# Queueing a block's gate product on VectorE behind that block's own low part

## The chip, the cores and the metric

The kernel runs on one core of a Trainium2 chip. The metric is the device time of one execution in microseconds. Three runs of the kernel before gave 3089.33 to 3090.34 us, median 3090.05 us.

## What is computed

Two small network blocks run one after the other on 256 tokens of width 1024. Each ends, and the second has twice, a "PEER" layer: every token picks 16 of 16384 experts in each of 8 heads, and an expert is a pair of rows, one of a table u and one of a table v.

```python
e = (i1 * PEER_NKEYS + i2).reshape(TOK_BLOCK, PEER_HEADS * K)
gate = jax.nn.softmax(best_s, axis=-1).reshape(TOK_BLOCK, PEER_HEADS * K)
u = expert_u[e]
act = jax.nn.gelu(jnp.einsum('td,ted->te', xb, u), approximate=False)
coef = (gate * act.astype(jnp.float32)).astype(xb.dtype)
return jnp.einsum('te,ted->td', coef, expert_v[e])
```

Between the three PEER layers lie token mixers (a convolution with an RWKV scan, a gated linear attention, a stick-breaking attention), norms and residuals. All is float32.

## The kernel before, in words

**PEER as two dense products.** The kernel does not gather experts. It computes the activation of all 16384 experts for all 256 tokens and multiplies it by a gate that is zero where a token did not pick the expert. In `peer` (L1049) this is done in blocks of 128 experts. The *up stage* (loop at L1189, 128 blocks) multiplies a block of u with the tokens into the PSUM tile `pu`, and ScalarE's Gelu (L1197) writes the result to `C`, an SBUF tile with 256 columns per block. The *down stage* (`vstep`, L1209, and `acc_nat`, L151, 128 blocks) multiplies `C` with the block of v and adds up into the four PSUM tiles `py`, two halves of the tokens by two halves of the width.

**Float32 by three products.** Every streamed operand is split in two parts: `hi`, a rounded copy made by ScalarE (L79 for weights, L106 for activations, where it is called `ch`), and `lo`, the rest, made by VectorE as raw minus hi (L81; L107, called `cl`). A product is hi by hi, hi by lo and lo by hi. In the down stage these are, per block and per tile of `py`, ch by hi (L162), ch by lo (L163) and cl by hi (L164): 12 products of 128x512 per block.

```python
raw = self.sp.tile([128, n], F32, tag="raw", name="raw", bufs=RAW)
nc.sync.dma_start(raw, ap)
...
nc.scalar.copy(hi, raw)
with self.behind():
    self.los.append(nc.vector.tensor_tensor(lo, raw, hi.bitcast(F32), op=OP.subtract))
```

This is `stream` (L72): one block of a table comes by a DMA of SP's queue (512 KB, four `raw` buffers), and `hi` and `lo` have three buffers each, as have `ch` and `cl` in the down stage. `self.los` keeps every lo instruction.

**The gates.** They are found during the up stage by work that is interleaved with it. For the tokens 128 to 255 the gate is multiplied into `C` in the up stage (L1136, L1201). For the tokens 0 to 127 the gates are added into a table `G` in HBM by 128 indirect DMAs on GpSimd (L1097), and the down stage reads it back: for every four blocks `vstep` loads a tile `gate` of 256 KB on GpSimd's queue (L1212, two buffers), and VectorE multiplies it into the first 128 columns of the block in `C` (L1215). This *gate product* must come before the block's ch and cl.

**What sets the order.** A scheduler orders each engine's instructions when the program is built; an engine then runs its own list strictly in order and waits by semaphores. `tc.issue_after(x)` tells the scheduler to put the instructions of its body behind x on their engine. Before, x is `done`, the last lo of the up stage. The last three blocks of the down stage (`TAIL`, L169) are worked off tile by tile of `py`, so that its four tiles finish one after the other.

**Around the stages.** Behind the first and the second down stage come the mixers: SP's queue loads the old residual (`res`, L676) and the mixer's first weights, and GpSimd's queue loads rows for the norm (`rowg`, `rowb`, L669); VectorE adds `py` to `res` (L688, L714). Behind the third one there is only the last norm (L714 to L722) and the output.

Of the kernel before, what the change touches and what calls it, by code (L numbers as in the profile page):

```python
# [39 lines left out]
class Net:  # L40
# [1008 lines left out]
    def peer(self, xh, xl, wq, skT, uT, v, G, Gnext=None, rate=1.5, dve_a=2):  # L1049
# [5 lines left out]
        nc, tc = self.nc, self.tc  # L1055
        V = nc.vector
        NS = 88
        with ExitStack() as ctx:
# [19 lines left out]
            def after(i):  # L1078
                for j in last:
                    tc.add_manual_dep(i.ins, j.ins.name, SYNC, reason="adds of the head before")  # L1080
# [123 lines left out]
            py = [self.ps.tile([128, 512], F32, tag="y", name="py", bufs=4) for i in range(4)]  # L1204
            Gv = G.rearrange("(p b t) o -> p b (t o)", p=128, t=128)
            gate = [None]
            done = self.los[-1]

            def vstep(b):  # L1209
                if b % 4 == 0:  # L1210
                    gate[0] = wp.tile([128, 4, 128], F32, tag="A", name="gate")
                    after(nc.gpsimd.dma_start(gate[0], Gv[:, b:b + 4]))  # L1212
                hi, lo = self.stream(v[b])
                with tc.issue_after(done.ins):
                    V.tensor_tensor(C3[:, b, :128], C3[:, b, :128], gate[0][:, b % 4], op=OP.mult)  # L1215
                ch = wp.tile([128, 256], F32R, tag="ch", name="ch", bufs=TAIL)
                cl = wp.tile([128, 256], F32R, tag="cl", name="cl", bufs=TAIL)
                self.split(ch, cl, C3[:, b])
                return ch, cl, hi, lo
            self.acc_nat(py, range(128), vstep)  # L1220
        return py

# [158 lines left out]
def build(nc, tc, a):  # L1381
    with ExitStack() as ctx:
# [15 lines left out]
        n.block1(a, *x)  # L1398
        nc.gpsimd.dma_start(n.vec2, a["vec2"])
        py = peer(0, x)  # L1400
        x, y = xt(), xt()

        def first_a(fp):
            s = n.load_res(fp, hs[0])
            n.add_rms(fp, s, py, n.rows(fp, a["g_final_row"], "g"), *x, norm=True)
            return s
        n.mixer_a(a, first_a, *x, *y, hs[1])
        py = peer(1, y)
        x, y = xt(), xt()

        def first_b(fp):
            s = n.load_res(fp, hs[1])
            n.add_ln(fp, s, py, a, (0, 1), *x)
            return s
        n.mixer_b(a, first_b, *x, *y, hs[2])
        py = peer(2, y)
        with tc.tile_pool(name="fc", bufs=1) as fp:
            n.add_ln(fp, n.load_res(fp, hs[2]), py, a, (1, 1), dst=a["out"])
# [17 lines left out]
```

## Time and profile before

| | |
|---|---|
| median of three runs | 3090.05 us (3089.33 to 3090.34) |
| the profiled execution's own time | 3088.2 us |
| its span, first to last instruction | 3086.4 us |
| mean granted TensorE clock | 0.987 |
| TensorE products, busy | 2982.7 us (97%), 21313 |
| VectorE, busy | 2101.8 us (68%), 4439 |
| ScalarE, busy | 1621.3 us (53%), 3016 |
| gate product L1215 | 384 of 286 ns, 90.6 us |
| lo L81 | 939, 1141.3 us |
| hi L79 | 939, 978.1 us |

A timeline row gives the start, the duration, the engine, the line and what is written from what; in brackets stands how long the engine had been idle and what ended that. "PE" is TensorE's products, "PEld" its weight loads, which run ahead of the products, "DVE" VectorE, "ACT" ScalarE, "POOL" GpSimd. Products overlap: one of 128x512 has a duration of 0.39 us in the rows, and the next one starts 0.23 us after it. So TensorE can be late without an idle time in its row.

### The profile page before, as it was taken

The numbers are of one execution on the slowest core, as the hardware profiler recorded it, in microseconds if no ns is written. First come the engines' busy times: TensorE is split into PE (matmuls) and PEld (weight loads), VectorE is DVE, ScalarE is ACT, GpSimd is POOL, SyncE is SP. The second block draws the span as 40 slices with busy tenths as digits, with TensorE's granted clock in tenths as the row PEclk, the third lists the DMA queues.
The fourth block names the chain that finished last, engine by engine and source line by source line (L and its number), as shares of the span: only waits on it lengthen the run. The fifth ranks groups of instructions, "written<-read, shape, count | busy, mean of one in ns | idle before, by whom it ended". The sixth has DMA issues, their size and how long they took to land. (4 is left out here: it accounts for less than half of the span.)

```text
span 3086.4 us, 56042 instructions
## 1 busy us (share of the span) xinstructions
PE 2982.7 (97%) x21313; PEld 2716.2 (88%) x21313; DVE 2101.8 (68%) x4439; ACT 1621.3 (53%) x3016; POOL 857.2 (28%) x564
## 2 busy tenths in 40 slices
PE   9999999999899999999999999998999999989998
PEld 8888999999688888899999878887889999978887
DVE  6976997545766665798744666665599764476666
ACT  6345558544455454456844444455544774444554
POOL 0000067884100010008788100000002878610000
PEclk9999999999999999999999999999999999999999
DMA  9745566666756653456666666655345666676665
GB/s 313 231 142 194 178 163 139 171 183 208 244 192 194 195 179 116 156 174 157 144 179 185 231 219 194 195 193 174 112 158 176 147 150 185 190 238 211 194 193 176
DMA packets 231918, 568.83 MB, mean 184 GB/s; under 512 B 74416, under 2 KB 99264, under 8 KB 231392
## 3 DMA queue, kind: packets, MB, share of 16 engines
q1 hardware_dynamic: 165536, 529.31, 52.4%
q0 software_dynamic: 66112, 35.94, 8.2%
q8 instruction: 167, 2.74, 0.4%
q14 instruction: 103, 0.84, 0.1%
HBM read 533.49 MB, written 31.65 MB: 183 GB/s over the span
## 5 line engine op out<-in xcount | busy, mean ns | idle before, releaser
L81 DVE TENSOR_TENSOR lo<-raw,hi 128x1024 fp32r<-128x1024 f32 (+1 forms) x939 | 1141.3, 1216 | 558.3 <-ACT hi L79 553.1
L79 ACT CAST hi<-raw 128x1024 fp32r<-128x1024 f32 (+1 forms) x939 | 978.1, 1043 | 691.0 <-PE pu L112 274.3
L1097 POOL DMA_INDIRECT G<-gts,idx x384 | 774.4, 2017 | 525.2 <-issue 140.2
L111 PE MATMUL pu<-xh,hi 128*128 128x256 f32 x3072 | 879.0, 286 | 3.0 <-ACT hi L79 3.0
L113 PE MATMUL pu<-xh,lo 128*128 128x256 f32 x3072 | 874.2, 285 | 7.4 <-DVE lo L81 7.4
L112 PE MATMUL pu<-xl,hi 128*128 128x256 f32 x3072 | 871.2, 284 | 0.0
L163 PE MATMUL py<-lo,ch 128*128 128x512 f32 x1536 | 602.6, 392 | 32.0 <-DVE lo L81 32.0
L113 PEld LDWEIGHTS pu<-xh,lo 128*128 128x128 f32 x3072 | 590.9, 192 | 11.9 <-DVE lo L81 10.5
L164 PE MATMUL py<-hi,cl 128*128 128x512 f32 x1536 | 598.6, 390 | 0.0
L162 PE MATMUL py<-hi,ch 128*128 128x512 f32 x1536 | 598.5, 390 | 0.0
L111 PEld LDWEIGHTS pu<-xh,hi 128*128 128x128 f32 x3072 | 591.0, 192 | 3.6 <-ACT hi L79 3.6
L112 PEld LDWEIGHTS pu<-xl,hi 128*128 128x128 f32 x3072 | 591.4, 193 | 0.0
L106 ACT CAST ch<-C 128x256 fp32r<-128x256 f32 x384 | 156.1, 407 | 557.6 <-PE py L163 552.1
L163 PEld LDWEIGHTS py<-lo,ch 128*128 128x128 f32 x1536 | 288.7, 188 | 106.9 <-DVE lo L81 47.5
L162 PEld LDWEIGHTS py<-hi,ch 128*128 128x128 f32 x1536 | 288.4, 188 | 61.2 <-ACT hi L79 0.9
L164 PEld LDWEIGHTS py<-hi,cl 128*128 128x128 f32 x1536 | 288.7, 188 | 58.6
L107 DVE TENSOR_TENSOR cl<-C,ch 128x256 fp32r<-128x256 f32 x384 | 162.5, 424 | 162.1 <-ACT ch L106 162.1
L669 POOL DMA_DIRECT2D rowg<-in_ln_rows_dram x4 | 2.2, 551 | 580.9 <-DVE cl L107 560.9
L111 PE MATMUL pz<-xh,hi 128*128 128x256 f32 (+1 forms) x504 | 149.6, 298 | 8.5 <-ACT hi L79 6.1
L113 PE MATMUL pz<-xh,lo 128*128 128x256 f32 (+1 forms) x504 | 147.3, 293 | 1.1 <-DVE lo L81 1.1
L112 PE MATMUL pz<-xl,hi 128*128 128x256 f32 (+1 forms) x504 | 146.7, 291 | 0.5 <-DVE xl L214 0.5
L1215 DVE TENSOR_TENSOR C<-C,gate 128x128 f32<-128x128 f32 x384 | 90.6, 286 | 65.5 <-DMA gate<-G 65.4
(490 smaller groups left out, 3605.3 us busy)
## 6 DMA issues: line engine op xcount, KB each, us to landing
raw<-in_u_dram SPq DMA_DIRECT2D x384, 512.0 KB
raw<-in_v_dram SPq DMA_DIRECT2D x384, 512.0 KB
G<-zero SPq DMA_DIRECT2D x96, 256.0 KB
raw<-in_wq_dram SPq DMA_DIRECT2D x48, 512.0 KB
gate<-G POOLq DMA_DIRECT2D x96, 256.0 KB
raw<-in_w_in_dram SPq DMA_DIRECT2D x38, 512.0 KB
raw<-in_a_w_inT_dram SPq DMA_DIRECT2D x14, 512.0 KB
raw<-in_b_wT_dram SPq DMA_DIRECT2D x14, 512.0 KB
```

The costliest lines, as they stand in the source:

```text
L79: nc.scalar.copy(hi, raw)
L81: self.los.append(nc.vector.tensor_tensor(lo, raw, hi.bitcast(F32), op=OP.subtract))
L106: nc.scalar.copy(hi, src)
L107: nc.vector.tensor_tensor(lo, src, hi.bitcast(F32), op=OP.subtract)
L111: mm(out, lh, rh, start=start, stop=False)
L112: mm(out, lh, rl, start=False, stop=False)
L113: mm(out, ll, rh, start=False, stop=stop)
L162: mm(po[q], xh[:, ts], hi[:, h], start=f, stop=False)
L163: mm(po[q], xh[:, ts], lo[:, h], start=False, stop=False)
L164: mm(po[q], xl[:, ts], hi[:, h], start=False, stop=l)
L1097: i = nc.gpsimd.indirect_dma_start(G, bass.IndirectOffsetOnAxis(ap=idx[:, k:k + 1], axis=0), gts[:, k:k + 1], None, compute_op=OP.add)
L1215: V.tensor_tensor(C3[:, b, :128], C3[:, b, :128], gate[0][:, b % 4], op=OP.mult)
```

## The change

The gate product of block b is put behind the lo of block b, which `stream` has just appended to `self.los`, in place of the last lo of the up stage:

```diff
@@ -1204,14 +1204,13 @@
             py = [self.ps.tile([128, 512], F32, tag="y", name="py", bufs=4) for i in range(4)]
             Gv = G.rearrange("(p b t) o -> p b (t o)", p=128, t=128)
             gate = [None]
-            done = self.los[-1]
 
             def vstep(b):
                 if b % 4 == 0:
                     gate[0] = wp.tile([128, 4, 128], F32, tag="A", name="gate")
                     after(nc.gpsimd.dma_start(gate[0], Gv[:, b:b + 4]))
                 hi, lo = self.stream(v[b])
-                with tc.issue_after(done.ins):
+                with tc.issue_after(self.los[-1].ins):
                     V.tensor_tensor(C3[:, b, :128], C3[:, b, :128], gate[0][:, b % 4], op=OP.mult)
                 ch = wp.tile([128, 256], F32R, tag="ch", name="ch", bufs=TAIL)
                 cl = wp.tile([128, 256], F32R, tag="cl", name="cl", bufs=TAIL)
```

One line goes, so that all later lines have a number less by one: the gate product, L1215 before, is L1214 in the changed kernel. What the scheduler makes of it is shown at three places. The numbers behind the names tell buffers' tiles apart; each block has its own.

The start of the first down stage on VectorE, before; lo_9887 and lo_9910 are those of the down stage's blocks 0 and 1 (L1201 still belongs to the up stage):

```order
L1201 TENSOR_TENSOR C_3873<-C_3873,act_9770 128x128
L1215 TENSOR_TENSOR C_3873<-C_3873,gate_9882 128x128 x4
L107 TENSOR_TENSOR cl_9892<-C_3873,ch_9891 128x256
L1215 TENSOR_TENSOR C_3873<-C_3873,gate_9976 128x128 x3
L81 TENSOR_TENSOR lo_9887<-raw_9884,hi_9886 128x1024
L1201 TENSOR_TENSOR C_3873<-C_3873,act_9805 128x128
L107 TENSOR_TENSOR cl_9915<-C_3873,ch_9914 128x256
L107 TENSOR_TENSOR cl_9938<-C_3873,ch_9937 128x256
L1215 TENSOR_TENSOR C_3873<-C_3873,gate_9976 128x128
L1215 TENSOR_TENSOR C_3873<-C_3873,gate_10070 128x128 x3
L81 TENSOR_TENSOR lo_9910<-raw_9907,hi_9909 128x1024
```

The same place in the changed kernel, behind lo_9887; lo_9933 and lo_9956 are those of blocks 2 and 3:

```order
L1201 TENSOR_TENSOR C_3873<-C_3873,act_9805 128x128
L1214 TENSOR_TENSOR C_3873<-C_3873,gate_9882 128x128
L107 TENSOR_TENSOR cl_9892<-C_3873,ch_9891 128x256
L81 TENSOR_TENSOR lo_9910<-raw_9907,hi_9909 128x1024
L1201 TENSOR_TENSOR C_3873<-C_3873,act_9840 128x128
L1214 TENSOR_TENSOR C_3873<-C_3873,gate_9882 128x128
L107 TENSOR_TENSOR cl_9915<-C_3873,ch_9914 128x256
L1201 TENSOR_TENSOR C_3873<-C_3873,act_9875 128x128
L81 TENSOR_TENSOR lo_9933<-raw_9930,hi_9932 128x1024
L1214 TENSOR_TENSOR C_3873<-C_3873,gate_9882 128x128
L81 TENSOR_TENSOR lo_9956<-raw_9953,hi_9955 128x1024
L107 TENSOR_TENSOR cl_9938<-C_3873,ch_9937 128x256
```

Before, eleven gate products of three gate tiles stand ahead of the second block's lo; now each block has one, and from the third block on cl of a block stands behind lo of the block after it (cl_9938 is block 2's).

ScalarE further on in the first down stage, before; ch_10054, ch_10079 and ch_10102 are those of blocks 7, 8 and 9, hi_10049, hi_10074, hi_10097 and hi_10120 those of blocks 7 to 10:

```order
L106 CAST ch_10054<-C_3873 128x256
L79 CAST hi_10049<-raw_10047 128x1024
L106 CAST ch_10079<-C_3873 128x256
L79 CAST hi_10074<-raw_10072 128x1024
L106 CAST ch_10102<-C_3873 128x256
```

And in the changed kernel:

```order
L106 CAST ch_10054<-C_3873 128x256
L79 CAST hi_10097<-raw_10095 128x1024
L106 CAST ch_10079<-C_3873 128x256
L79 CAST hi_10120<-raw_10118 128x1024
L106 CAST ch_10102<-C_3873 128x256
```

Before, ch of a block came ahead of its own hi; now hi of block 9 comes ahead of ch of block 8. This pattern holds to the end of each down stage.

The end of the first down stage on VectorE, before; cl_12851 and lo_12846 belong to the last block, meml and res to the mixer:

```order
L107 TENSOR_TENSOR cl_12840<-C_3873,ch_12839 128x256
L81 TENSOR_TENSOR lo_12835<-raw_12832,hi_12834 128x1024
L107 TENSOR_TENSOR cl_12851<-C_3873,ch_12850 128x256
L81 TENSOR_TENSOR lo_12846<-raw_12843,hi_12845 128x1024
L107 TENSOR_TENSOR meml_12908<-memr_12909,memh_12907 128x1024
```

And in the changed kernel:

```order
L81 TENSOR_TENSOR lo_12846<-raw_12843,hi_12845 128x1024
L107 TENSOR_TENSOR cl_12840<-C_3873,ch_12839 128x256
L1214 TENSOR_TENSOR C_3873<-C_3873,gate_12796 128x128
L107 TENSOR_TENSOR cl_12851<-C_3873,ch_12850 128x256
L107 TENSOR_TENSOR meml_12908<-memr_12909,memh_12907 128x1024
```

The last cl has moved behind the last lo, the cl of the block before and the last gate product; the third down stage ends in the same order. On SP's queue at the first stage's end, before (a_w_mk and a_w_mv are the mixer's first weights, res the residual):

```order
L75 DMA raw_12918<-in_a_w_mk_dram 128x1024
L676 DMA res_13047<-h0_90 128x1024
L75 DMA raw_12950<-in_a_w_mk_dram 128x1024
L75 DMA raw_12985<-in_a_w_mv_dram 128x1024
L75 DMA raw_13015<-in_a_w_mv_dram 128x1024
L676 DMA res_13049<-h0_90 128x1024
```

And in the changed kernel:

```order
L75 DMA raw_12918<-in_a_w_mk_dram 128x1024
L75 DMA raw_12950<-in_a_w_mk_dram 128x1024
L676 DMA res_13047<-h0_90 128x1024
L676 DMA res_13049<-h0_90 128x1024
L75 DMA raw_12985<-in_a_w_mv_dram 128x1024
L75 DMA raw_13015<-in_a_w_mv_dram 128x1024
```

The two loads of the residual have come together, behind both loads of the first weight.

## Rows read from the trace of the kernel before

**Rows 1.** TensorE's longest wait of the whole program (engine, line, waited for: us, times, longest us).
```profile
PE py L163 <- DVE lo L81: 32.0, 34, 2.2
```

**Rows 2.** Busy time by stretch: the three down stages (columns named in its head).
```profile
core 0: us, PE busy (x) PEld busy (x) DVE busy (x) ACT busy (x) POOL busy (x), PEclk, DMA share, GB/s
750.31:1104.72 354.41, 343.48 (x1503) 280.64 (x1501) 226.96 (x369) 170.09 (x252) 15.02 (x28) 1.00 0.64 207
1729.48:2084.76 355.28, 344.00 (x1503) 280.52 (x1501) 227.36 (x369) 170.10 (x252) 15.03 (x28) 1.00 0.63 207
2713.07:3067.70 354.63, 344.80 (x1502) 281.80 (x1501) 227.19 (x369) 170.34 (x252) 15.02 (x28) 1.00 0.63 204
sum 1064.32, PE 1032.29 PEld 842.95 DVE 681.50 ACT 510.53 POOL 45.07; mean PE 344.10 PEld 280.98 DVE 227.17 ACT 170.18 POOL 15.02
```

**Rows 3.** The same view: an early and a late stretch of the first down stage.
```profile
760.00:860.00 100.00, 89.07 (x380) 69.98 (x379) 72.00 (x169) 42.18 (x63) 12.88 (x24) 1.00 0.72 238
900.00:1000.00 100.00, 100.00 (x443) 82.77 (x442) 60.43 (x74) 50.38 (x74) 0.00 (x0) 1.00 0.60 193
```

**Rows 4.** Timeline of VectorE (start us, us, instruction, [idle before <-releaser]), before a stall.
```profile
760.39 0.50 DVE L1215 TENSOR_TENSOR C<-C,gate 128x128 f32<-128x128 f32 x2 [1.16 <-DMA gate<-G]
760.80 1.22 DVE L81 TENSOR_TENSOR lo<-raw,hi 128x1024 fp32r<-128x1024 f32 x1
```

**Rows 5.** Timeline of TensorE's weight loads at that stall.
```profile
762.08 0.19 PEld L163 LDWEIGHTS py<-lo,ch 128*128 128x128 f32 x1 [0.89 <-DVE lo L81]
```

**Rows 6.** The gate product's line, what it waited for (us, times).
```profile
  DMA gate<-G: 65.4, 46
```

**Rows 7.** Timeline of TensorE, undisturbed blocks and two later places.
```profile
952.17 0.39 PE L164 MATMUL py<-hi,cl 128*128 128x512 f32 x1
952.40 0.39 PE L162 MATMUL py<-hi,ch 128*128 128x512 f32 x1
...
1104.72 0.39 PE L162 MATMUL py<-hi,ch 128*128 128x512 f32 x1
...
2091.62 0.39 PE L164 MATMUL py<-hi,cl 128*128 128x512 f32 x1
```

**Rows 8.** The chain that ended last (start us, us, what): the longest gate transfer on it.
```profile
2685.95 6.63 DMA gate<-G
```

**Rows 9.** Timeline of ScalarE, an undisturbed block and the second stage's end.
```profile
952.68 1.05 ACT L79 CAST hi<-raw 128x1024 fp32r<-128x1024 f32 x1
...
2092.04 1.05 ACT L79 CAST hi<-raw 128x1024 fp32r<-128x1024 f32 x1 [4.06 <-PE py L164]
```

**Rows 10.** Timeline of VectorE, an undisturbed block and the first stage's end.
```profile
952.81 0.42 DVE L107 TENSOR_TENSOR cl<-C,ch 128x256 fp32r<-128x256 f32 x1 [0.54 <-ACT ch L106]
953.76 1.22 DVE L81 TENSOR_TENSOR lo<-raw,hi 128x1024 fp32r<-128x1024 f32 x1 [0.53 <-ACT hi L79]
...
1106.08 1.23 DVE L81 TENSOR_TENSOR lo<-raw,hi 128x1024 fp32r<-128x1024 f32 x1 [0.53 <-ACT hi L79]
1107.23 1.22 DVE L107 TENSOR_TENSOR meml<-memr,memh 128x1024 fp32r<-128x1024 f32 x1
```

**Rows 11.** Timeline of TensorE's weight loads, undisturbed.
```profile
952.63 0.19 PEld L164 LDWEIGHTS py<-hi,cl 128*128 128x128 f32 x1
```

**Rows 12.** Timeline of TensorE's products: the one behind the stalled one.
```profile
762.42 0.40 PE L164 MATMUL py<-hi,cl 128*128 128x512 f32 x1
```

**Rows 13.** The same chain, at the end of the third down stage.
```profile
3068.11 0.44 DVE cl L107
3068.57 3.23 DMA res<-h
3071.92 1.28 DVE res L714 x2
```

**Rows 14.** Timeline of TensorE behind the first and the second down stage.
```profile
1115.57 0.39 PE L111 MATMUL pz<-memh,hi 128*128 128x256 f32 x1 [2.24 <-ACT hi L79]
...
2097.74 0.58 PE L111 MATMUL pz<-memh,hi 128*128 128x256 f32 x1 [4.09 <-ACT hi L79]
```

## The prediction, made before the changed kernel ran

> **What bounds the kernel now.** Look first at who makes TensorE wait. The longest entry of its waits is the product with the block's low part: 34 waits, 32.0 us, all for VectorE's lo [rows 1]. They lie in the down stages, so the next view is the busy time of the three down stages, each taken from its first product to the first product of its last three blocks (125 blocks) [rows 2]: 354.41, 355.28 and 354.63 us. The granted clock is 1.00 in all three. Then compare two stretches inside a stage: from 760 to 860 us TensorE is busy 89.07 of 100 us, from 900 to 1000 us all of it [rows 3]. The loss is thus at the stage's start, where the gate products run.
>
> The mechanism is in VectorE's timeline around one stall: two gate products had to wait 1.16 us for their gate transfer, and behind them in VectorE's queue stood a lo that waited for nothing else; it ended at 760.80 + 1.22 = 762.02 us [rows 4]. TensorE's weight load for the product with that lo starts at 762.08 us [rows 5]. In the whole program gate products waited 65.4 us for gate transfers, 46 times [rows 6]. Before the change, products of later blocks are queued as early as a scheduler finds room, and a product that nobody needs yet holds up a lo that TensorE needs now.
>
> An undisturbed block takes 2.72 us: from 952.40 to 1104.72 us are 56 blocks, 152.32 / 56 [rows 7]. 125 blocks without a stall are 340.0 us, three stages 1020.0; measured are 1064.32 [rows 2]. So the stalls and the restarts behind them cost **44.3 us**, more than the 32.0 us of idle time, since each also delays the products behind it.
>
> **The change, part by part.** Nothing is added or removed: 384 gate products, 96 gate transfers, all casts stay. Their places move.
>
> *Products.* Each product now stands behind its own block's lo, and so block by block through the stage. A product has the gate of its four blocks loaded while the buffer before is used up: two buffers, so a transfer may be issued once the last product of a group is done, and is needed five blocks later, 5 x 2.72 = 13.6 us. The longest gate transfer on the chain took 6.63 us [rows 8]. I cost gate waits at nothing; the cover is 7 us. DMA load: gate bytes no longer come in a burst of 238 GB/s [rows 3] but spread at 256 KB per four blocks, 10.9 us, some 24 GB/s on top of the 193 of the quiet stretch [rows 3], 217 in all. That is less than the burst carried, so nothing. Gain: 44.3 us, if nothing takes the stalls' place.
>
> *The order that the scheduler now makes.* This is where the gain can be lost. Before, a block's ch and cl are made first and its hi and lo after. Now ScalarE makes hi of block b+1 ahead of ch of block b, and VectorE lo of b+1 ahead of cl of b. hi has three buffers, so hi of b+1 can start only when TensorE has finished block b-2. I follow that chain from S, the start of block b-1's first product:
> - TensorE's last product of b-2 starts 0.23 us before S (952.17 against 952.40 [rows 7]); a hi that waited for such a product started 0.42 us after its start (2091.62 [rows 7], 2092.04 [rows 9]). hi of b+1 starts at S + 0.19.
> - hi to lo, start to start: 952.68 [rows 9] to 953.76 [rows 10], 1.08. lo of b+1 starts at S + 1.27.
> - lo to the next instruction: 1106.08 to 1107.23, 1.15 [rows 10]. cl of b starts at S + 2.42 and takes 0.42 (the row at 952.81 [rows 10]): S + 2.84. Its ch is done before: behind hi, at about S + 1.56.
> - VectorE's end to TensorE's weight load 0.06 (762.02 to 762.08 [rows 4, 5]): usable at **S + 2.90**.
> - Due: block b starts at S + 2.72, and the weight load of cl 0.23 later (952.63 [rows 11] against 952.40), **S + 2.95**. It may be late by a little: undisturbed the matmul after its own starts 0.45 us behind it (952.40 + 3 x 0.227 = 953.08), behind the late load at 762.08 it started at 762.42 [rows 12], 0.34. So 0.11 us are hidden, and the limit is S + 3.06.
>
> The chain fits by 0.16 us. Before there was more than a block of reserve: the lo that ended at 953.76 + 1.22 = 954.98 [rows 10] was for the block that starts at 952.40 + 2 x 2.72 = 957.84. I take no stall per block. Below, the bound is that same zero (TensorE cannot run faster than 2.72); above, each 0.1 us by which the chain passes the limit costs 375 x 0.1 = 37.5 us.
>
> The Trainium skill, "VectorE: DVE Perf Modes", section "The DRAIN you can't avoid", says that after each instruction the next one does not start until the pipe is empty (it adds that one that is not held starts earlier). The trace disagrees with the strict reading: the instruction behind the lo at 1106.08 started 0.08 us before that lo's end at 1107.31 [rows 10]. By the strict rule cl would be usable at S + 2.98, the sum would stay, half the margin would be gone, and I would give the slower rival 0.2 in place of what it has below.
>
> *Last blocks.* For the last block ch waits for the product, and the product now stands behind lo and behind cl of the block before: S + 2.84, then about 0.2 for the product, 0.5 for ch, 0.45 for cl, end near S + 3.93, S now the start of the last three blocks (3067.70 in the third stage [rows 2]). Before it ended at 3068.54, S + 0.84 [rows 13]. TensorE orders its last products to suit; I add 0.3 us a stage, 1 in all. But the residual's load waits for that cl (its tile takes C's place), and at the end of the program this is on the chain: cl, 3.23 us of transfer, then VectorE to the end without a pause [rows 13]. So the end comes 3.93 - 0.84 = **3.1 us** later.
>
> *The two inner stage ends.* The same delay meets other cover there. TensorE stood idle 2.24 and 4.09 us before products of the next stage, for a hi of its first weights [rows 14], whose transfers shared SP's queue with the residual's. Now the second of these weight transfers is queued ahead of the residual's. Between a loss of 3.1 us each and a gain of what was idle (6.3 in all) I take a gain of 2 in all, since that order favours it.
>
> **Sum**: -44.3 + 1 + 3.1 - 2 = -42.2 us, against the profiled execution's 3088.2 us 3046.0. The median of the runs is 1.85 us above that execution: **3048 us**. A measurement of this kernel tells about 0.2% from no change, 6 us: under 3084 is faster, over 3096 slower.
>
> **Rivals.**
> 1. *A gap in every block (slower).* Place: TensorE's product with cl. Mechanism: hi of b+1 waits for TensorE to free block b-2, and cl of b comes only behind lo of b+1. It decides when the chain is longer than worked out by 0.16 + 42.2/375 = 0.27 us. For: the margin is the sum of five short steps. Against: each step was read from a row, and in the quiet stretch nothing disturbed them [rows 3]. With a gap of 0.2 us: 3048 + 75 = 3123. The Trainium skill, "Perfetto Trace Analysis", section "Optimization Strategy", says that the same gap, repeated on the engine that should be saturated, can mean too little room for the next tile; no row of before shows such a gap, and here the room would be the three hi buffers.
> 2. *Small gaps.* The same chain 0.02 to 0.1 us past its limit, or raw data now and then late with no reserve left: half the gain, about 3067 (3056 to 3084).
> 3. *Nothing gained.* The lo are late for another reason, or the products now wait for gates once per group: 3090. Against: outside the burst there is not one stall [rows 3], and a gate has 13.6 us. That the products are not moved is excluded by the order of the built program.
>
> **How the numbers follow.** Forecast 0.62 (3041 to 3056: the stage ends may each give 3 us more or less), small gaps 0.18, nothing 0.07, a gap in every block 0.13. Faster 0.80, within 0.2% 0.07, slower 0.13. The range of 8 in 10 takes in the forecast and the small gaps: 3041 to 3084.
>
> **What would show it.** In the changed profile: no wait of the product with lo in the down stages; three stages of 340 to 341 us from the first product to the last three blocks; each gate product directly behind a lo and cl pair, with no wait for a gate transfer; cl ending some 0.1 us before its weight load; the residual's load at the end 3 us later against the last blocks. Wrong it would be if waits of the product with cl appear, 0.1 us or more in hundreds, or if the gate products wait once in four blocks.

## The result and the profile after

| | before | after |
|---|---|---|
| median of four runs | 3089.69 us (3086.62 to 3090.34) | 3051.69 us (3049.45 to 3051.92) |
| span of the profiled execution | 3086.4 us | 3047.6 us |
| TensorE products, busy | 2982.7 us (97%) | 2973.8 us (98%) |

The ratio is 0.9877 (95% interval 0.9860 to 0.9894): 38.0 us or 1.2% less, clear of the noise, inside the predicted range of 3041 to 3084 and 3.7 us above the predicted 3048. The profiled execution was the fastest of the four (3049.45 us); the spans differ by 38.8. All lines from 1207 on have a number lower by one than before.

The busy time of the three down stages, each from its first product to the first product of its last three blocks (the same stretches as in [rows 2], same columns), and an early stretch as in [rows 3]:

```profile
750.39:1090.42 340.03, 340.03 (x1503) 281.54 (x1501) 220.27 (x376) 169.84 (x252) 16.09 (x30) 1.00 0.69 216
1713.45:2053.48 340.03, 340.03 (x1503) 281.54 (x1502) 220.27 (x376) 169.75 (x252) 16.10 (x30) 1.00 0.67 217
2683.57:3024.18 340.61, 340.61 (x1502) 281.31 (x1501) 220.26 (x376) 169.80 (x252) 16.09 (x30) 1.00 0.67 213
...
760.00:860.00 100.00, 100.00 (x443) 82.81 (x442) 65.10 (x111) 49.55 (x74) 4.83 (x9) 1.00 0.69 217
```

The stages lost 354.41 - 340.03, 355.28 - 340.03 and 354.63 - 340.61, together 43.65 us; TensorE is busy all through them. The gate product's line says why: under "sat idle before it" stands nothing, where 65.4 us of waits for gate transfers stood [rows 6], and it is now the gate transfers that wait for products.

```profile
L1214 DVE TENSOR_TENSOR C<-C,gate x384: 280/284/286, 747.1 to 3027.0; 128x128 f32<-128x128 f32 x192
its engine sat idle before it (us, times) until:
who waited for it (us, times):
  POOL gate L1211: 982.7, 90
```

A steady block, on ScalarE, VectorE and among TensorE's products and weight loads (timelines; the block that uses this cl starts at 954.42, the one before it at 951.70):

```profile
951.94 1.05 ACT L79 CAST hi<-raw 128x1024 fp32r<-128x1024 f32 x1 [1.36 <-issue]
952.90 0.40 ACT L106 CAST ch<-C 128x256 fp32r<-128x256 f32 x1
...
953.03 1.23 DVE L81 TENSOR_TENSOR lo<-raw,hi 128x1024 fp32r<-128x1024 f32 x1 [0.96 <-ACT hi L79]
954.17 0.42 DVE L107 TENSOR_TENSOR cl<-C,ch 128x256 fp32r<-128x256 f32 x1
954.51 0.28 DVE L1214 TENSOR_TENSOR C<-C,gate 128x128 f32<-128x128 f32 x1
...
951.70 0.39 PE L162 MATMUL py<-hi,ch 128*128 128x512 f32 x1
...
954.65 0.19 PEld L164 LDWEIGHTS py<-hi,cl 128*128 128x128 f32 x1
```

The order is the predicted one, and cl ends at 954.17 + 0.42 = 954.59: with the 0.06 us from VectorE to a weight load [rows 4, 5] it is usable at 954.65, just when the load is due. The chain has nothing to spare there.

What was gained in the stages was partly given back at the program's end (the chain that ended last, then VectorE):

```profile
3027.80 0.44 DVE cl L107
...
3028.63 7.02 DMA res<-h
...
3031.77 1.29 DVE L714 SCALAR_TENSOR_TENSOR res<-res,py 128x512 f32<-128x512 f32 x2 [3.54 <-DMA res<-h]
3035.74 0.69 DVE L714 SCALAR_TENSOR_TENSOR res<-res,py 128x512 f32<-128x512 f32 x1 [1.50 <-DMA res<-h]
```

From the first product of the last three blocks to the end it was 3086.4 - 3067.70 = 18.7 us; now it is 3047.6 - 3024.18 = 23.4. The last cl ends at 3028.23, 4.05 us after that product, where it was 0.84 [rows 13]. Then VectorE waits twice for the residual, 3.54 and 1.50 us. Before, it waited once (VectorE before):

```profile
3071.92 1.28 DVE L714 SCALAR_TENSOR_TENSOR res<-res,py 128x512 f32<-128x512 f32 x2 [1.62 <-DMA res<-h]
```

The whole difference of the two profiled spans, by stretches (us; the last three blocks of an inner stage are taken up to 0.23 us, one product's distance, behind the start of its last product):

| stretch | before | after | difference | predicted |
|---|---|---|---|---|
| start to first down stage | 750.31 | 750.39 | +0.1 | 0 |
| 125 blocks, three stages | 1064.32 | 1020.67 | -43.65 | -44.3 |
| last three blocks, first two stages | 8.45 + 8.44 | 8.55 + 8.52 | +0.2 | +0.7 |
| between down stages 1 and 2, 2 and 3 | 616.31 + 619.87 | 614.48 + 621.57 | -0.1 | -2 |
| last three blocks of stage 3, to the end | 18.70 | 23.42 | +4.7 | +3.4 |
| sum | 3086.4 | 3047.6 | -38.8 | -42.2 |

### The profile page after: what moved, and what is told of

Read it like the earlier page. It is cut to its first block, busy times and chain, and to the rows that moved or that the text cites. A ratio compares the mean times of both kernels' runs of the same rounds, so it can differ in the third digit from the quotient of the medians.

```text
span 3047.6 us, 55671 instructions
## 1 busy us (share of the span) xinstructions
PE 2973.8 (98%) x21313; PEld 2719.7 (89%) x21313; DVE 2077.3 (68%) x4439; ACT 1619.5 (53%) x3016; POOL 865.6 (28%) x564
## 4 chain that ended last, share of the span: by engine, by line
PE 87%; DVE 9%; ACT 2%; issue 1%; DMA 1%; POOL 0%; DVEq 0%; ACTq 0%; SPq 0%; POOLq 0%
PE pu L113 11%; PE py L164 11%; PE py L162 11%; PE py L163 11%; PE pu L112 11%; PE pu L111 11%; PE pg L1131 3%; DVE lo L81 2%; PE pz L113 2%; PE pz L111 2%; PE pz L112 2%; DVE acc L340 1%; PE pq L113 1%; PE pq L112 1%; PE pq L111 1%
## 5 line engine op out<-in xcount | busy, mean ns | idle before, releaser
L1097 POOL DMA_INDIRECT G<-gts,idx x384 | 782.3, 2037 | 532.0 <-DVE gts L1090 236.3
L1211 POOL DMA_DIRECT2D gate<-G x96 | 51.9, 541 | 993.1 <-DVE C L1214 971.1
L1197 ACT ACTIVATE C<-pu 128x128 f32<-128x128 f32 (+13 forms) x384 | 119.3, 312 | 0.2
```

The lines of the kernel that those rows point to most:

```text
L1097: i = nc.gpsimd.indirect_dma_start(G, bass.IndirectOffsetOnAxis(ap=idx[:, k:k + 1], axis=0), gts[:, k:k + 1], None, compute_op=OP.add)
L1197: nc.scalar.activation(C3[:, b, :tm], pa[:, :tm], AF.Gelu)
```

## Experiments

The theory: before, a lo was late because products stood ahead of it in VectorE's queue and waited there for gate transfers; the changed order removes that, costs nothing in a steady block, and moves the last cl and with it the residual's load. Its rivals: contention by the burst of gate bytes; products queued too early, whatever they wait for; a late end that comes from the transfers' own traffic; a chain with more, or with no, reserve. The kernel before was timed beside each group of four kernels: 3080.80, 3081.50 and 3082.51 us there, 7 to 9 us lower than 3089.69, so groups are compared by their ratios and by stretches of their profiles. No profile of the kernel before was taken beside them, so it is open which of its stretches is shorter there. E1 and E2 lie 36.9 and 37.0 us below it, less than the 44 us by which their three stages lie below the earlier profile's.

### E1: no gate transfers to wait for

```
-                if b % 4 == 0:
+                if b == 0:
                     gate[0] = wp.tile([128, 4, 128], F32, tag="A", name="gate")
```

> The kernel before, but a down stage loads one gate tile at its first block and all its 128 products read that one; the other 31 gate transfers of the stage are left out (so the gate table's values are left out but for four blocks). The order of the products stays the scheduler's. Theory (the loss of before is VectorE's queue standing behind products that wait for gate transfers): no such waits, so the three stages, first product to last three blocks, come to 340 to 341 us each and the time to 3089.7 - 44 = about 3046 us. Rival (the loss is products queued ahead of their need, whatever they wait for): the products still stand ahead of lo, the stages stay at 350 or more, about 3085 us.

3043.92 us (3042.82 to 3046.70), ratio 0.9884 (0.9867 to 0.9900). The three stages:

```profile
750.54:1090.57 340.03, 340.03 (x1502) 281.61 (x1501) 226.55 (x367) 169.96 (x252) 0.00 (x0) 1.00 0.58 193
1713.92:2053.95 340.03, 340.03 (x1502) 281.70 (x1501) 226.53 (x367) 169.92 (x252) 0.00 (x0) 1.00 0.57 193
2683.56:3023.59 340.03, 340.03 (x1503) 281.70 (x1501) 226.56 (x367) 170.13 (x252) 0.00 (x0) 1.00 0.57 190
```

The products still run ahead: VectorE is busy 76.87 us between 760 and 860 us with 167 instructions, against 169 before [rows 3]. Products that run ahead in the scheduler's order cost nothing by themselves. The rival "too early, whatever they wait for" falls.

### E2: the same burst of transfers, but nothing reads them

```
-                if b % 4 == 0:
+                if b == 0:
                     gate[0] = wp.tile([128, 4, 128], F32, tag="A", name="gate")
                     after(nc.gpsimd.dma_start(gate[0], Gv[:, b:b + 4]))
+                elif b % 4 == 0:
+                    t = wp.tile([128, 4, 128], F32, tag="B", name="unread")
+                    after(nc.gpsimd.dma_start(t, Gv[:, b:b + 4]))
```

> As the one before, but all gate transfers are made, at the pace of the queue, into tiles that nothing reads; the products read the first gate tile alone (the gate table's values are left out but for four blocks). Theory (waits of the products in VectorE's queue): nothing waits for the transfers, so again 340 to 341 us a stage and about 3046 us. Rival (contention: the burst of gate bytes makes the v transfers late): the burst is there as before or denser, so the stages stay near 354 us and the time near 3085 to 3090.

3043.76 us (3041.47 to 3047.05), ratio 0.9883. An early stretch of the first stage and the whole stage:

```profile
760.00:860.00 100.00, 100.00 (x443) 82.84 (x442) 76.83 (x166) 49.87 (x74) 8.75 (x17) 1.00 0.71 241
...
750.30:1090.33 340.03, 340.03 (x1503) 281.66 (x1501) 226.55 (x367) 169.91 (x252) 10.96 (x21) 1.00 0.63 210
```

The burst is there, 241 GB/s against 238 in the kernel before [rows 3], and TensorE is busy all the time, where it was busy 89.07 us of 100. Contention falls too. With E1 it is shown that the loss was the wait of products, standing in VectorE's queue ahead of lo.

### E3 and E10: the product behind the third last lo

```
-                with tc.issue_after(self.los[-1].ins):
+                with tc.issue_after(self.los[-3].ins):
```

> The changed kernel, but a block's product stands behind the lo two blocks before its own (the third last instead of the last). Theory: the order cl of a block, then the next lo, comes back, with a block of reserve and no gate wait (the buffers give 13.6 us, two blocks less are 8 us, the transfers take under 7): stages of 340.0 us; the last cl ends some 3 us earlier against the last blocks, so the residual's load is again hidden behind TensorE's last products and the end is 18.7 us behind the last three blocks instead of 23.4; the inner stage ends go back to those of before (one 1.8 us longer, one 1.7 shorter). About 3046 to 3047 us against 3051.7. Rival (the late end comes from the transfers' own traffic, not from the last cl): the end stays at 23 us, about 3051. Rival (gate waits come back): stages of 345 or more, 3060 and up.

3046.71 us (3043.47 to 3048.57), ratio 0.9893. VectorE's order in a steady block of E3:

```profile
949.26 0.29 DVE L1214 TENSOR_TENSOR C<-C,gate 128x128 f32<-128x128 f32 x1
949.89 0.43 DVE L107 TENSOR_TENSOR cl<-C,ch 128x256 fp32r<-128x256 f32 x1 [0.34 <-ACT ch L106]
950.85 1.23 DVE L81 TENSOR_TENSOR lo<-raw,hi 128x1024 fp32r<-128x1024 f32 x1 [0.53 <-ACT hi L79]
```

cl stands ahead of the next lo again, ch ahead of hi, no product waits for a gate, and each stage takes 340.02 us:

```profile
750.85:1090.87 340.02, 340.02 (x1502) 281.53 (x1501) 231.42 (x376) 170.61 (x251) 16.09 (x30) 1.00 0.64 217
```

The end takes 3041.7 - 3022.88 = 18.8 us, as before the change.

To set it against the changed kernel, both ran once more together:

> The changed kernel as it is, beside the next two on one chip. Stages of 340.0 to 340.6 us and an end of 23.4 us from the first product of the last three blocks; 614.5 us between the first down stage and the second, 621 to 623 between the second and the third, as in its first profile. About 1.2% below the kernel before.

> The product behind the third last lo, again, beside the changed kernel on the same chip. If only the end differs (18.8 us against 23.4) and the stretches between the stages cancel (2 us longer after the first down stage, 2 to 3 shorter after the second): 4 to 5 us below the changed kernel, 0.15%. If the stretches between the stages don't cancel: 2 to 8 us below it. If the order in a stage costs something that the stages' lengths hide: not below it.

The changed kernel: 3053.16 us (3048.90 to 3057.51, five runs), ratio 0.9906 (0.9889 to 0.9922); stages of 340.03, 340.03 and 340.59, an end of 23.5, as expected. It gains 29.4 us there, 0.9%, not the expected 1.2%: the kernel before is 7 us lower than in the first comparison, the changed one 1.5 higher. The stretches between the stages missed the expectation, 616.1 and 624.2 us instead of 614.5 and 621 to 623. The third last lo: 3045.27 us (3043.36 to 3047.69, four runs), ratio 0.9884 (0.9868 to 0.9899); stages of 340.02, 340.02 and 340.03, an end of 18.9. It is 7.9 us lower, at the upper end of the 2 to 8 us that were expected if the stretches between the stages differ, and all its runs lie below all of the other's. The profiled spans differ by 3051.3 - 3041.5 = 9.8 us: 4.6 are the end, 0.6 the third stage, 2.4 lie between the stages (below), and 2.2 before the first down stage, where the two do the same. So 5.2 us have a cause in this document, and the other 4.6 are of the size by which profiles of one kernel differ. By the medians this version is below both kernels.

### E4: the product behind the second last lo

> The changed kernel, but a block's product stands behind the lo of the block before its own. cl of a block then stands behind its own lo, one block earlier than in the changed kernel. Theory: stages of 340.0 us; the last cl ends about 1.1 us earlier against the last blocks (one lo and a product less in the chain), so the end is about 22.3 us instead of 23.4; about 3050.5 us. Rival (as above): no change of the end, 3051.7.

3047.29 us (3046.05 to 3051.73), ratio 0.9896. The stages are 340.03, and the last cl ends at 3028.31, 2.89 us after the first product of the last three blocks (3025.42), 1.16 earlier than in the changed kernel, as expected. The end, however, is 20.8 us, not the expected 22.3: the second residual tile took 5.47 us on the chain, not 7.02, so VectorE's second wait shrank to 0.17 us. The cl's move was right, the residual's second tile was not thought of.

### E7: only the last cl is moved

```
-                with tc.issue_after(self.los[-3].ins):
+                with tc.issue_after(self.los[-3 if b < 125 else -1].ins):
```

> The kernel with the product behind the third last lo, except that the products of a stage's last three blocks stand behind their own lo. It moves the last cl alone. Theory: stages of 340.0 us as before, but the end takes 23 to 23.5 us from the first product of the last three blocks, as in the changed kernel, instead of 18.8; about 4.6 us slower than the kernel with all products behind the third last lo. Rival (the late end comes with the order in the whole stage, or from traffic): the end stays at 18.8.

3048.54 us (3045.11 to 3053.37), ratio 0.9889: 2 us above E3's median from another group, where 4.6 were expected; among runs that spread like these the time shows neither. The profile is clear: stages of 340.03, and an end of 3051.6 - 3028.41 = 23.2 us, on the chain:

```profile
3031.91 0.44 DVE cl L107
3032.74 6.89 DMA res<-h
```

So the last three products of a stage are enough for the late end: they move the last cl from 0.88 us (E10) to 3.92 us behind the first product of the last three blocks, and the residual's load with it. That is the predicted mechanism. The rest of the end's growth is the second residual tile, which E8 turns to.

### E8: 512 KB less beside the residual

```
-        brow = self.rows(pool, a["ln_rows"][(l * 2 + j) * 2 + 1], "b")
+        brow = grow if xh is None else self.rows(pool, a["ln_rows"][(l * 2 + j) * 2 + 1], "b")
```

> The changed kernel, but the last normalisation loads one row tile in place of two and uses it for both (the additive row's values are left out), so 512 KB less are loaded beside the residual at the end. Theory (the end waits for the second residual tile, which shares the transfer engines with the two row tiles): 2 MB took 7.0 us, 1.5 MB take about 5.3, so VectorE's second wait for the residual (1.50 us) goes and the end is about 1.5 us shorter, 22 us instead of 23.4. Rival (the end is set by the first residual and VectorE's work alone): no change, 23.4.

3050.79 us (3047.57 to 3051.11), ratio 0.9896. The end is 3048.9 - 3027.33 = 21.6 us; VectorE there:

```profile
3034.66 1.28 DVE L714 SCALAR_TENSOR_TENSOR res<-res,py 128x512 f32<-128x512 f32 x2 [3.28 <-DMA res<-h]
3035.86 1.28 DVE L715 BATCH_NORM_STATS2 lnst<-res 128x6 f32<-128x512 f32 x2
3037.05 0.67 DVE L714 SCALAR_TENSOR_TENSOR res<-res,py 128x512 f32<-128x512 f32 x1
```

The second wait is gone and the end is 1.8 us shorter, while the first wait stays. So the part of the end that the prediction missed is the second residual tile, which lands late while it shares the transfers with the row tiles. That part does not hang on the late cl. E11 (below) has the early cl at its end and the same second wait, and its end takes 20.3 us instead of E10's 18.9:

```profile
3026.98 6.98 DMA res<-h
...
3034.05 0.69 DVE L714 SCALAR_TENSOR_TENSOR res<-res,py 128x512 f32<-128x512 f32 x1 [1.60 <-DMA res<-h]
```

E5 and E6 (next) have the late cl and no second wait; there both residual tiles are issued ahead of the row tiles, and the end takes 22.0 us.

### E5 and E6: how much room the chain has

```
-                self.split(ch, cl, C3[:, b])
+                nc.scalar.copy(ch, C3[:, b])
+                pad = wp.tile([128, 32], F32, tag="pad", name="pad", bufs=1)
+                V.tensor_copy(pad, ch[:, :32].bitcast(F32))
+                V.tensor_tensor(cl, C3[:, b], ch.bitcast(F32), op=OP.subtract)
```

E6 has 128 in place of 32.

> The changed kernel plus one copy of 128x32 (from ch to a scratch tile) on VectorE in every block, between lo of the next block and cl, so it lengthens the steady chain hi, lo, cl by the copy. From the rows of the 128x128 product (0.28 us) and the 128x256 cl (0.42), less 0.08 of overlap, it adds about 0.10 us. If the margin is the 0.16 us of the prediction: no gap, stages of 340.0 us, no change against the changed kernel. If it is 0.08 to 0.09, as three blocks of the changed kernel's third stage say (hi 0.28 us late, 0.19 us lost each): 0.01 to 0.02 us a block, stages of 341 to 343 us, 4 to 8 us slower. If there were no reserve at all: 0.10 x 375 = 37 us slower.

> As the one before, with a copy of 128x128, which adds about 0.20 us to the chain by the same rows. Margin 0.16: 0.04 us a block, stages of 345 us, 15 us slower than the changed kernel. Margin 0.08 to 0.09: 0.11 to 0.12 us a block, stages of 354 to 355 us, 41 to 45 us slower. If the chain were not what a late cl hangs on (another reserve takes it up): stages of 340, no change.

E5: 3056.03 us (3053.21 to 3061.48), ratio 0.9922. E6: 3056.07 us (3053.47 to 3058.39), ratio 0.9914. The copies put 0.08 us (952.34 to 952.42) and 0.14 us (949.90 to 950.04) between lo and cl. VectorE in E5, then in E6:

```profile
952.34 0.17 DVE L1219 COPY pad<-ch 128x32 f32<-128x32 f32 x1
952.42 0.42 DVE L1220 TENSOR_TENSOR cl<-C,ch 128x256 fp32r<-128x256 f32 x1
```

```profile
949.90 0.22 DVE L1219 COPY pad<-ch 128x128 f32<-128x128 f32 x1
950.04 0.42 DVE L1220 TENSOR_TENSOR cl<-C,ch 128x256 fp32r<-128x256 f32 x1
```

The stages, E5 first, E6 second:

```profile
746.46:1090.23 343.77, 343.77 (x1502) 280.27 (x1501) 230.84 (x501) 169.68 (x252) 16.09 (x30) 1.00 0.65 214
1712.46:2056.20 343.74, 343.74 (x1502) 280.13 (x1501) 230.83 (x501) 169.68 (x252) 16.10 (x30) 1.00 0.65 214
```

```profile
752.76:1095.39 342.63, 342.63 (x1503) 274.23 (x1502) 236.91 (x501) 169.78 (x252) 16.12 (x30) 1.00 0.67 215
1717.63:2060.43 342.80, 342.80 (x1502) 274.29 (x1501) 236.92 (x501) 169.69 (x252) 16.14 (x30) 1.00 0.65 215
```

The first two stages of each are shown; the third took 344.26 us in E5 and 343.64 in E6, against 340.6 in the changed kernel. Neither expectation is met. E5 loses 3.7 us a stage, 0.03 us a block, though 0.08 lies well inside a margin of 0.16. For a margin of 0.08 to 0.09 it is near the expected 341 to 343 us, but E6 is far from the 354 to 355 that go with that margin. E6 loses 2.6 to 3.0 us a stage, 0.02 a block, less than the shorter copy. Its weight loads for cl wait 43 times in the 125 blocks of the first stage (engine, line, waited for: us, times, longest):

```profile
PEld py L164 <- DVE cl L1220: 6.9, 43, 0.2
```

Two things can be read. First, the chain is at its limit: both copies cost, and not their full length. Second, lateness that is "hidden" is not quite free: in E5's first two stages no wait of TensorE is listed, but in many blocks products follow each other every 0.231 us in the mean instead of 0.2267, and a block takes 2.72 to 2.78 us from hi to hi. Why the shorter copy costs more is open.

### E12: the longer copy, with a block of reserve

> The product behind the third last lo, plus the 128x128 copy between ch and cl in every block, which cost the changed kernel 2.6 to 3.6 us a stage. Theory: here cl stands ahead of the next lo and has a block of reserve, so the 0.14 us that the copy adds to VectorE's order in a block cost nothing: stages of 340.0 us. Rival (the copy costs through VectorE's load or a memory port, wherever it stands): stages of 342.6 to 343.7 again.

3043.37 us (two runs only, 3042.86 and 3043.88), ratio 0.9875. The copy runs in every block, ahead of cl as in E6, and the stage does not notice:

```profile
953.15 0.23 DVE L1219 COPY pad<-ch 128x128 f32<-128x128 f32 x1 [0.34 <-ACT ch L1217]
953.29 0.42 DVE L1220 TENSOR_TENSOR cl<-C,ch 128x256 fp32r<-128x256 f32 x1
...
751.38:1091.41 340.03, 340.03 (x1502) 281.54 (x1501) 248.57 (x500) 170.79 (x251) 16.14 (x30) 1.00 0.64 217
```

With VectorE busier than in any other version shown (248.57 us), the same instruction costs nothing where cl stands a block earlier. What E5 and E6 measured is the chain of the changed order, not VectorE's load.

### E11: one inner stage end in each order

```
-                with tc.issue_after(self.los[-3].ins):
+                with tc.issue_after(self.los[-3 if b < 125 or self.layer else -1].ins):
...
+            self.layer += 1
```

(self.layer counts the layers from zero.)

> The product behind the third last lo, but in the first of the three down stages the last three blocks' products stand behind their own lo, so that the residual's load stands behind the second weight transfer of the next stage there, as in the changed kernel. If the 2 us that the kernels with a late last cl are faster between the first and the second down stage come from that order: 614.5 us there instead of 616.5 to 617, and 2 us below the kernel before it in this list. If they are a difference between runs: no change.

3044.61 us (3042.12 to 3047.77), ratio 0.9876 (0.9860 to 0.9892). Between the first and the second down stage are 614.6 us, against 616.7 in E10, the expected 2 us. But the changed kernel itself, with the same order there, took 616.1 in E9, and the medians of E11 and E10 differ by 0.7 us, less than the runs of either spread. So neither that the 2 us come from the order nor a gain in time is shown.

## Why the prediction was right, and where its terms were off

**The stalls, -44.3: right, -43.65.** Mechanism and size held; E1 and E2 show the mechanism apart from its rivals. The 0.6 us that are missing are in the third stage, where ScalarE starts a hi 0.28 us late three times, 87.2 us (32 blocks) apart, and the chain passes it on (ScalarE, then the weight load):

```profile
2773.88 1.05 ACT L79 CAST hi<-raw 128x1024 fp32r<-128x1024 f32 x1 [1.64 <-issue]
...
2776.57 0.19 PEld L164 LDWEIGHTS py<-hi,cl 128*128 128x128 f32 x1 [0.31 <-DVE cl L107]
```

This is the rival "small gaps", at three of 384 blocks. The version with reserve has 340.03 us in that stage.

The late hi is no matter of the third stage alone. The trace also records ScalarE's wait instructions, which the timeline leaves out, and with them the same pause of 0.28 us stands in every stage: at 854.54, 941.58 and 1028.62 in the first, each 128 ScalarE instructions (32 blocks) behind the last one. There it falls ahead of a wait that ends later anyway, in the third stage between that wait and hi.

**Gate waits at nothing, gate bytes at nothing: right.** No product waits for a gate; the stage moves 216 GB/s, 217 were worked out.

**The chain: right in its order, too short by 0.05 us in its first step.** With S at 951.70, hi of block b+1 starts at S + 0.24, not S + 0.19: the 0.42 us from TensorE's last product to a hi that waited for it were read at a stage's end [rows 7, 9]; in the stage they are 0.47 (951.47 to 951.94). The steps behind it agree within 0.01. cl is usable at S + 2.95, exactly when due, and only the 0.11 us of hidden lateness are left of the 0.16. On that count a hi 0.28 us late should cost 0.17, and cost 0.58 / 3 = 0.19; E6, 0.03 us past the limit, should cost 3.8 us a stage and cost 2.6 to 3.0. E5, 0.03 us inside it, should have cost nothing and cost 3.7: "hidden" held for a single late load, not for one in every block. So the limit of the prediction, though the change itself came through, does not describe a chain that is late in every block; what does is open.

The Trainium skill, "VectorE: DVE Perf Modes", section "The DRAIN you can't avoid", read strictly, would have put cl 0.08 us later still. The trace disagrees again: cl at 954.17 starts 0.09 us before the lo ahead of it ends (953.03 + 1.23). E5, where cl does start 0.08 us later, lost 3.7 us a stage.

**The rival "a gap in every block" did not come, but its place was right.** E5 and E6 show how near it was: 0.14 us more in the chain, and TensorE waits for cl. The room that is missing can be had without more buffers: one block earlier in VectorE's order (E12). The Trainium skill, "Perfetto Trace Analysis", section "Optimization Strategy", says that the same gap, repeated, can mean too little room for the next tile. E6's weight loads, which wait at the same place 43 times in 125 blocks, are such a gap, but E12 shows that with the same buffers the order alone closes it.

**Last blocks, +0.3 a stage: +0.1.** 8.45 us became 8.55.

**The program's end, +3.1: mis-sized, +4.7 with the last blocks in it.** The last cl came about when worked out (S + 4.05 against 3.93; the steps listed for it add up to 3.99), and the first addition of the residual moved by 3.4 us. The step that failed is "3.23 us of transfer, then VectorE to the end without a pause": it was read from the first residual tile alone. In the changed kernel the second tile ends the last wait, 7.02 us after its issue, and adds 1.50 us of idle time. E8 takes that away, and E11 shows it with the early cl too, so only some 3.2 of the 4.7 us are the late cl's.

**The two inner stage ends, -2: not found.** TensorE's idle time in the first products of the next stage went from 2.24 us [rows 14] and 1.38 behind it to 0.44 + 1.99 at the first, from 4.09 [rows 14] + 0.22 to 0.45 + 2.30 at the second. The weights' order helped hi, and lo of the same weights became the wait. And at the second the residual's later arrival shows behind it: the waits of the transposes for the normalised residual grew, before first, after second (whole program; the growth is one wait at the second end, 0.71 to 3.41 us):

```profile
PE ptr L199 <- DVE res L722: 9.7, 5, 3.3
```

```profile
PE ptr L199 <- DVE res L722: 12.4, 5, 3.4
```

That wait is 2.9 to 3.7 us in all seven profiles whose second stage has the product behind its own or the second last lo at its end, and at most 0.71 in the other seven. So what the term left out is this wait behind the normalisation. What both ends make together stays open. The stretches between the stages sum to 1236.2 us before, 1236.0 after and 1240.3 in E9; 1234.9, 1237.9 and 1234.9 with the third last lo (E3, E10, E12). They vary by some 4 us between runs of one kernel, as much as the term is worth.

**Where it was lucky.** The gain in the stages and the late end came by the mechanisms that were worked out. But the chain fitted with nothing to spare where 0.16 us were counted on, of which 0.05 were misread: 0.08 us more (E5) would have cost some 11 us over the three stages, without any wait that points to it.

## What to carry to other kernels

In an engine's in-order list an instruction that waits holds up all behind it, here 65.4 us of waits before and none after: place work that waits for a transfer behind what the bound engine needs next, and not before its data is due. But moving it later also moves what depends on it: look at the steady order that results (here cl fell behind the next lo and lost a block of reserve) and at the last iteration, whose end releases the next stage's loads. Two blocks earlier in the queue kept the whole gain in the stages and the last cl where it was before, and came out 0.26% below the change itself by the medians.

## What the runs showed of the hardware that was not expected

- A copy of 0.17 us that put 0.08 us into the chain cost TensorE more (343.8 us a stage) than one that put in 0.14 (342.6). With loads that arrive just in time, TensorE's products were 0.231 us apart instead of 0.2267 in many blocks, with no wait listed. The cause is open.
- ScalarE pauses 0.28 us every 128 of its instructions in all three down stages of the changed kernel (first stage 854.54, 941.58, 1028.62; third 2773.88, 2861.14, 2948.36). Some 2 us behind each an 8 KB packet starts on the instruction queue q14 (856.41, 943.35, 1030.47; 2776.17, 2863.20, 2950.45). That loading ScalarE's instructions makes the pause is a guess. Where it falls decides what it costs: nothing in two stages, 0.19 us each time in the third.
- The second residual tile took 5.5 to 5.8 us on the chain in E2, E3, E4 and E10 and 6.9 to 7.1 in the changed kernel (twice), E7 and E11, with the same bytes to load. The DMA packets tell the groups apart. In the second one the row tiles' first packet starts 0.1 to 0.2 us before the last packet of the first residual tile starts, in the first one 0.5 to 0.7 us behind it. What sets that order was not tested.
